# A 256-token hybrid block on one core: diagonal blocks of 32 rows solved on VectorE in place of 16, and side work handed out in larger turns

## The chip, the cores and the metric

One core of a Trainium2 chip runs one launch of the kernel. The metric is the device time of that launch in microseconds. The kernel before has a median of 1571.18 us over 3 runs (1570.76 to 1572.39). Engines are called by the profile's short names: PE is TensorE (PEld its weight load), DVE is VectorE, ACT is ScalarE, POOL is GpSimd, SP is SyncE.

## What is computed

One layer on 256 tokens of width 2048, all in float32. Branch A is a gated delta rule in chunks of 64 rows with 8 heads of width 128; branch B is latent attention with 8 heads; then an output projection, an MLP of width 8192 and a gated embedding. Cut to the part that the change touches:

```python
h = rms_norm(x) ; proj = h @ w_in            # q|k|v|z|beta|alpha, MLA parts, gates
q, k, v = silu(causal_conv(...)) ; q, k = l2norm(q), l2norm(k)
a = where(strict, (k*beta) @ k.T * decay, 0)       # per head and chunk
t_inv = triangular_solve(eye + a, eye)             # lower triangular inverse
w, u = t_inv @ (k*beta*exp(gc)), t_inv @ (v*beta)
# scan over chunks: v_new = u - w @ state; o = q @ state + qk @ v_new; ...
y = sigmoid(g_a) * (o_a @ w_branch_a) + sigmoid(g_b) * (o_b @ w_branch_b)
x = x + y @ w_out
x = x + relu(rms_norm(x) @ w_mlp_up)**2 @ w_mlp_down
x = x + sigmoid(rms_norm(x) @ w_ple_gate) * (p @ w_ple)
```

## The kernel before

**The stream.** Nearly all of PE's time goes to the large weight matrices. `stream` walks through a list of groups; a group is one block of 512 (or fewer) weight columns, and a step is two K tiles of 128 rows of it. Each weight tile is loaded by SP (`raw`, 5 buffers), cut by `cut` into a rounded part `whi` on ACT and a rest `wlo` on DVE (4 buffers each), and used in 12 matmuls per step (L425), or 8 of 512 and 8 of 256 columns in the groups of the up projection (L418 and L421). `cut(i + AHEAD)` with AHEAD = 3 stands at the head of step i, so a cut is written down three steps before its use, and its buffer comes free when the step four before it has been used.

**Side work.** Everything else (convolutions, norms, attention, the delta rule, transposes of activations) is written as generators in four lanes: L_MLA, L_CONV, L_SOLVE, L_TURN. Each `yield` ends a turn. After every step `weave()` is called twice; a call gives one turn to one lane, and a lane gets at most one turn in two calls, so about one per step. Where a step needs activations that are not written yet, `until` hands out turns at once. The order in which the instructions are written down is a priority: once `rx` is known, ACT and DVE are no longer held to it, and the framework puts each engine's instructions in an order by readiness under a model of its own.

**The inverse.** `inverse(half)` works on four heads and both token blocks `tb` of 128 rows (two chunks each). It computes `dt` (decay, bank `gr`) and the transposed `a` in `at`, then inverts I + a by blocks: the diagonal blocks of BASE = 16 rows are solved directly, and LEVELS = (16, 32, 64) doubles the block size three times. For the direct solve, `at` is masked and reduced on DVE to `ri`, sent by POOL's DMA queue to DRAM (`there`) and back as 64 blocks on 64 partitions (`blk`), solved row by row in 15 pairs of a multiply and a reduce on DVE, and sent through DRAM (`back`) to `ro`. At each level and for each tb, DVE makes `full` (tile `d`, the block columns spread over 128 columns) and `off` (tile `n`, masked `at`); PE makes four transposes (bank `te`, L949) and four float32 matmuls (bank `tx`, L954), then four more (bank `td`, L962 or L971); ACT copies `te` to `e` and `tx` to `xx`. A float32 matmul is two instructions on PE, a transpose is one: a turn with `te` and `tx` holds 4 + 8 instructions, a turn with `td` holds 8. `recur(half)` follows with 7 turns of matmuls, and `gated` turns the result into `oaT`, which the four groups of w_branch_a read.

**Buffers.** Tiles made by `big` share 23 slots of 4 KB per partition; PSUM has four banks for the stream (`acc`) and four for side work (`bank`).

**Where the turns end.** Before the change: `Acts.fill` ends a turn after two K tiles (one bank); `attention` after each query block's scores, and after each block's normalization; `conv` after each pair of heads and after each token block; `inverse` after each `gr`, each pair of `kk`, and each tb of each stage of a level. L_SOLVE thus takes 42 turns per half of the heads (6 to `at`, 3 for the way there, 5 for the solve, 3 for the way back, 18 for the levels, 7 for the recurrence).

Of the kernel before, what the change touches and what calls it, by code (L numbers as in the profile page):

```python
# [17 lines left out]
P = 128  # L18
# [19 lines left out]
C_GB = 8272  # L38
BASE = 16
LEVELS = (16, 32, 64)  # L40
NPIECE = 5
# [8 lines left out]
def _constants():  # L50

    i = np.arange(P)
    row, col = i[:, None], i[None, :]
    cols, at, n = [], {}, 0

    def put(name, a):
        nonlocal n
        a = np.broadcast_to(np.asarray(a, np.float32), (P, a.shape[-1]))
        at[name] = (n, n + a.shape[-1])
        n += a.shape[-1]  # L60
        cols.append(a)
# [10 lines left out]
    put("base", ((row // BASE == col // BASE) & (row < col)) * -1.0)  # L72
# [76 lines left out]
def hybrid_block(ctx: ExitStack, tc: tile.TileContext, a, dbg=None):  # L149
# [111 lines left out]
    class Acts:  # L261
# [18 lines left out]
        def fill(self, k0, src, scales=None):  # L280

            for j in range(src.shape[2] // (2 * P)):
# [18 lines left out]
                self.ready.update((k0 + 2 * j, k0 + 2 * j + 1))  # L301
                yield

# [352 lines left out]
    def evac_kv(g, ps):  # L656
# [30 lines left out]
    def attention(g):  # L687
        qn, qr, kn, v = (mla[c][g] for c in ("qn", "qr", "kn", "v"))
        prs = []
        for qb in range(NT):  # L690
# [17 lines left out]
            prs.append(pr)  # L708
            yield
            rs = small(2, "srs")  # L710
            dve.reciprocal(rs, sm)
            for e in range(2):
                dve.tensor_scalar(pr[:, e, :nk], pr[:, e, :nk], rs[:, e : e + 1], None, ALU.mult)
            yield
        pt0 = mid(f"pt0{g}", shape=(P, 2, T))
# [25 lines left out]
    def gates():  # L741
# [19 lines left out]
        for n in (15, 13, 11, 9, 7, 5, 3):  # L761
# [5 lines left out]
                                       ALU.mult, ALU.mult)  # L767
        yield
        ps = bank("gsum")[:, : 6 * NH].rearrange("p (b m h) -> p b m h", b=NT, m=3)
        for tb in range(NT):  # L770
# [15 lines left out]
    def conv(kind, half, ev):  # L786

        acc = big(f"cv{kind}{half}", shape=(P, 4, T))
        for pair in range(2):
# [5 lines left out]
            for e in range(2):  # L795
# [7 lines left out]
            yield  # L803
        y = acc
# [8 lines left out]
        for tb in range(NT):  # L813
# [8 lines left out]
            yield  # L822
        if kind in "qk":
# [8 lines left out]
        if kind in "kv":  # L832
            g[kind] = tm
        if kind == "k":
            kT = y
            for pair in range(2):
# [5 lines left out]
                act.copy(kT[:, 2 * pair : 2 * pair + 2, :].rearrange("p a b -> p (a b)"), tp)  # L842
                yield
            g["kT"] = kT
# [9 lines left out]
    def inverse(half):  # L854

        g = gdn[half]
        kT, qT = g["kT"], g["qT"]
        ats = []
        for tb in range(NT):
# [11 lines left out]
            act.activation(dt, dt, AF.Exp)  # L871
            yield
            at, qk = mid(f"at{half}{tb}"), mid(f"qk{half}{tb}")
            for pair in range(2):
# [6 lines left out]
                for e in range(2):  # L881
# [5 lines left out]
                    dve.tensor_tensor(qk[:, hs], ps[:, (2 * e + 1) * P : (2 * e + 2) * P], dt[:, hs], ALU.mult)  # L887
                yield
            g["qk", tb] = qk
# [8 lines left out]

        nb = P // BASE
# [6 lines left out]
        there = dpool.tile([NT, 4, P, BASE], F32, tag="there", name=f"there{half}")  # L906
        back = dpool.tile([NT, 4, P, BASE], F32, tag="back", name=f"back{half}")
        flat = lambda t: t.rearrange("b h (n j) i -> (b h n) j i", j=BASE)
        room = big(f"blk{half}", shape=(nblk, 3, BASE, BASE))
        blk, sol, prod = room[:, 0], room[:, 1], room[:, 2]  # L910
        for tb in range(NT):
            nc.gpsimd.dma_start(there[tb].rearrange("h p i -> p h i"), rows_in[:, tb])
        nc.gpsimd.dma_start(blk, flat(there))
        dve.memset(sol.rearrange("p i c -> p (i c)"), 0.0)
        dve.memset(sol.rearrange("p i c -> p (i c)")[:, 0 :: BASE + 1], 1.0)
        yield
        yield
# [7 lines left out]
        rows_out = mid(f"ro{half}", shape=(P, NT, 4, BASE), tag="ro", bufs=1)  # L925
        nc.gpsimd.dma_start(flat(back), sol)
        for tb in range(NT):
            nc.gpsimd.dma_start(rows_out[:, tb], back[tb].rearrange("h p c -> p h c"))
        yield
        yield  # L930
        yield


        cols = [rows_out[:, tb] for tb in range(NT)]
        inv_t, off, full, xx = [None] * NT, [None] * NT, [None] * NT, [None] * NT
        for b in LEVELS:
            for tb in range(NT):
                full[tb], off[tb] = mid(f"d{half}{tb}_{b}"), mid(f"n{half}{tb}_{b}")
                for h in range(4):
                    dve.tensor_tensor(  # L940
                        full[tb][:, h * P : (h + 1) * P].rearrange("p (n c) -> p n c", c=b),
                        cols[tb][:, h, :].unsqueeze(1).to_broadcast([P, P // b, b]),
                        C(f"bd{b}").rearrange("p (n c) -> p n c", c=b), ALU.mult)
                dve.tensor_tensor(v4(off[tb]), v4(ats[tb]), mask(f"lv{b}"), ALU.mult)
                yield
            for tb in range(NT):
                tp = bank(f"te{half}{tb}_{b}")
                for h in range(4):
                    pe.transpose(tp[:, h * P : (h + 1) * P], full[tb][:, h * P : (h + 1) * P], ident)  # L949
# [6 lines left out]
                act.copy(xx[tb], ps)  # L956
                yield
            for tb in range(NT):
# [9 lines left out]
                else:  # L968
# [5 lines left out]
                    g["inv_t", tb] = inv_t[tb]  # L974
                yield

# [299 lines left out]
```

## Time and profile before

| | |
|---|---|
| median of 3 runs | 1571.18 us |
| the profiled execution's own time | 1570.8 us |
| its span in the profile | 1569.0 us |
| PE, DVE, ACT, POOL busy in the span | 1559.6, 976.6, 775.7, 11.4 us |
| granted TensorE clock, mean | 0.999 |
| HBM traffic over the span | 181 GB/s |

The profile lists busy times per engine; since matmuls are pipelined, a busy PE says only that something was in flight. The chain of waits names, from the end backwards, what each piece of work followed; its rows give the start, the length and the number of instructions of a piece, and on PE the starts of successive pieces add up without overlap, so that a piece's length there is what it costs. Rows of groups give the count, the busy time of the group and, apart from it, the mean duration of one instruction, which on PE is a latency and longer than its share.

### The profile page before, as it was taken

The numbers are of one execution on the slowest core, as the hardware profiler recorded it, in microseconds if no ns is written. First come the engines' busy times: TensorE is split into PE (matmuls) and PEld (weight loads), VectorE is DVE, ScalarE is ACT, GpSimd is POOL, SyncE is SP. The second block draws the span as 40 slices with busy tenths as digits, with TensorE's granted clock in tenths as the row PEclk, the third lists the DMA queues.
The fourth block names the chain that finished last, engine by engine and source line by source line (L and its number), as shares of the span: only waits on it lengthen the run. The fifth ranks groups of instructions, "written<-read, shape, count | busy, mean of one in ns | idle before, by whom it ended". The sixth has DMA issues, their size and how long they took to land.

```text
span 1569.0 us, 20945 instructions
## 1 busy us (share of the span) xinstructions
PE 1559.6 (99%) x7856; PEld 1319.2 (84%) x7856; DVE 976.6 (62%) x1687; ACT 775.7 (49%) x1190; POOL 11.4 (1%) x23
## 2 busy tenths in 40 slices
PE   9999999999999999999999999999999999999998
PEld 7998888888888888888888888888888888888888
DVE  6987777954784655655665665556554665555554
ACT  6765776644534544444444443344433443445543
POOL 0000000100000000000000000000000000000000
PEclk9999999999999999999999999999999999999999
DMA  8564343444454455655555555555555555555563
GB/s 304 163 197 172 140 154 135 157 161 148 153 189 150 159 188 188 214 203 187 187 188 188 188 188 188 196 191 187 191 188 190 187 184 197 190 185 181 183 205 116
DMA packets 88518, 284.86 MB, mean 182 GB/s; under 512 B 9248, under 2 KB 22176, under 8 KB 88416
## 3 DMA queue, kind: packets, MB, share of 16 engines
q1 hardware_dynamic: 87168, 281.68, 52.6%
q10 hardware_dynamic: 864, 1.32, 0.3%
q8 instruction: 61, 1.00, 0.2%
q0 software_dynamic: 384, 0.53, 0.2%
q14 instruction: 41, 0.34, 0.1%
HBM read 281.13 MB, written 2.36 MB: 181 GB/s over the span
## 4 chain that ended last, share of the span: by engine, by line
PE 93%; DVE 3%; ACT 2%; DMA 1%; issue 1%; DVEq 0%; ACTq 0%
PE ps L425 65%; PE ps L418 15%; PE ps L421 8%; DMA raw<-in_weights 1%; DVE wlo L142 1%; PE tx L954 1%; ACT whi L142 1%; PE td L962 0%; DVE blk L142 0%; PE te L949 0%; DVE cvv L142 0%; ACT junk_k L142 0%; DMA first_x<-in_xT 0%; PE sc L696 0%; PE sc L695 0%
## 5 line engine op out<-in xcount | busy, mean ns | idle before, releaser
L142 DVE TENSOR_TENSOR wlo<-raw,whi 128x1024 fp32r<-128x1024 f32 (+3 forms) x541 | 644.1, 1192 | 499.8 <-ACT whi L142 497.4
L142 ACT CAST whi<-raw 128x1024 fp32r<-128x1024 f32 (+3 forms) x541 | 554.4, 1026 | 724.8 <-PE ps L425 494.7
L425 PE MATMUL ps<-whi,hT 128*128 128x512 f32 (+2 forms) x1344 | 424.1, 387 | 0.0
L425 PE MATMUL ps<-whi,uT 128*128 128x512 f32 x1024 | 320.4, 393 | 0.0
L425 PEld LDWEIGHTS ps<-whi,hT 128*128 128x128 f32 x1344 | 251.2, 188 | 42.5
L418 PE MATMUL ps<-nT,whi 128*128 128x512 f32 x1024 | 279.8, 394 | 0.0
L425 PE MATMUL ps<-wlo,hT 128*128 128x512 f32 (+2 forms) x672 | 256.8, 382 | 0.7 <-DVE wlo L142 0.7
L425 PEld LDWEIGHTS ps<-whi,uT 128*128 128x128 f32 x1024 | 191.9, 188 | 42.6
L425 PE MATMUL ps<-wlo,uT 128*128 128x512 f32 x512 | 200.8, 392 | 0.0
L418 PEld LDWEIGHTS ps<-nT,whi 128*128 128x128 f32 x1024 | 175.2, 188 | 23.1 <-DVE x L142 0.5
L421 PEld LDWEIGHTS ps<-nT,wlo 128*128 128x128 f32 x1024 | 157.1, 188 | 22.2
L421 PE MATMUL ps<-nT,wlo 128*128 128x256 f32 x1024 | 163.4, 281 | 0.0
L425 PEld LDWEIGHTS ps<-wlo,hT 128*128 128x128 f32 x672 | 126.6, 188 | 21.0 <-DVE wlo L142 1.0
L425 PEld LDWEIGHTS ps<-wlo,uT 128*128 128x128 f32 x512 | 96.2, 188 | 21.3
L425 PE MATMUL ps<-whi,gT 128*128 128x512 f32 (+1 forms) x320 | 82.3, 347 | 0.0
L425 PE MATMUL ps<-whi,yT 128*128 128x512 f32 x256 | 80.6, 393 | 0.0
L425 PEld LDWEIGHTS ps<-whi,gT 128*128 128x128 f32 x320 | 56.1, 189 | 7.5
L425 PEld LDWEIGHTS ps<-whi,yT 128*128 128x128 f32 x256 | 47.9, 189 | 9.5
L425 PE MATMUL ps<-wlo,gT 128*128 128x512 f32 (+1 forms) x160 | 55.5, 347 | 0.0
L425 PE MATMUL ps<-wlo,yT 128*128 128x512 f32 x128 | 50.2, 392 | 0.0
L425 PE MATMUL ps<-whi,oaT 128*128 128x512 f32 x128 | 40.7, 394 | 0.0
L425 PE MATMUL ps<-whi,obT 128*128 128x512 f32 x128 | 40.2, 392 | 0.0
(451 smaller groups left out, 1186.8 us busy)
## 6 DMA issues: line engine op xcount, KB each, us to landing
raw<-in_weights SPq DMA_DIRECT2D x492, 512.0 KB, 3.3
raw<-in_weights SPq DMA_DIRECT2D x24, 384.0 KB, 3.4
raw<-in_weights SPq DMA_DIRECT2D x16, 256.0 KB, 3.1
raw<-in_weights SPq DMA_DIRECT2D x7, 464.0 KB, 7.2
x<-in_x SPq DMA_DIRECT2D x4, 512.0 KB, 7.0
xT<-in_xT SPq DMA_DIRECT2D x7, 256.0 KB, 7.0
cst<-in_cst SPq DMA_DIRECT2D x1, 852.5 KB, 7.6
out<-sg SPq DMA_DIRECT2D x3, 256.0 KB, 2.8
```

Of the source, the lines that this page charges most:

```text
L142: i = f(*args, **kwargs)
L418: pe.matmul(ps[c], hi[:, j, cs], g.acts.both(k), start=first, stop=False)
L421: pe.matmul(ps[c][:, :T], lo[:, j, cs], g.acts.both(k)[:, :T], start=False, stop=last)
L425: pe.matmul(ps[tb], g.acts.at(k, part, tb), w[:, j, : g.n], start=(first and n_ == 0), stop=(last and n_ == 2),)
L954: pe.matmul(ps[:, h, :], off[tb][:, h * P : (h + 1) * P], cols[tb][:, h, :], start=True, stop=True)
```

## The change

BASE becomes 32 and LEVELS (32, 64). The direct solve now has 32 blocks of 32 rows; each block's 32 columns are split into four strips of STRIP = 8 columns, which fill 128 partitions. Per half, POOL's queue carries 8 writes of `at`'s diagonal blocks to DRAM, 4 loads (`room`), 4 writes of the result and 2 loads (`turned`), 18 in place of 6. ACT negates and turns the blocks (`flip`), and DVE runs 31 pairs of a multiply and a reduce over 8 columns. The result is transposed in 32x32 blocks by DVE (`cols`), and the spread and masked copy `inv_t` is made from `turned` on DVE, so that level 32 has no transposes on PE and level 16 is gone. The masks, the reduces to `ri` and two clearings are gone too.

Turns are merged: `fill` ends one after four K tiles; `attention` holds both query blocks; `conv` holds both pairs and both token blocks; `inverse` holds both `gr`, both pairs of a `kk`, and both token blocks of `td` and (level 32) of `tx`. One empty turn is added in `gates`, in `conv` of k and, between the normalization and the transposes, in `evac_kv`. L_SOLVE now takes 43 turns per half (1 + 2 to `at`, 5 for the way there, 1 for `flip`, 10 for the solve, 6 for the way back, 2 + 9 for the levels, 7 for the recurrence).

```diff
-BASE = 16
-LEVELS = (16, 32, 64)
+BASE = 32
+LEVELS = (32, 64)
+STRIP = 8
...
                 self.ready.update((k0 + 2 * j, k0 + 2 * j + 1))
-                yield
+                if j % 2 or 2 * j + 2 >= src.shape[2] // P:
+                    yield
...
-        rows_in = mid(f"ri{half}", shape=(P, NT, 4, BASE), tag="ri", bufs=1)
-        for tb in range(NT):
-            d = mid(f"db{half}{tb}")
-            dve.tensor_tensor(v4(d), v4(ats[tb]), mask("base"), ALU.mult)
-            dve.tensor_reduce(rows_in[:, tb], d.rearrange("p (h n c) -> p h c n", h=4, n=nb), AX.X, ALU.add)
...
+        for tb in range(NT):
+            for n in range(nb):
+                ns_ = slice(n * BASE, (n + 1) * BASE)
+                nc.gpsimd.dma_start(there[tb, :, n].rearrange("h j i -> j h i"), v4(ats[tb])[ns_, :, ns_])
+        room = big(f"blk{half}", shape=(P, BASE * BASE))
+        flip = big(f"flip{half}", shape=(P, BASE, BASE))
+        work = big(f"strip{half}", shape=(P, 2, STRIP, BASE))
+        sol, prod = work[:, 0], work[:, 1]
+        for c in range(ns):
+            nc.gpsimd.dma_start(room[c * nblk : (c + 1) * nblk], there.rearrange("b h n j i -> (b h n) (j i)"))
+        unit = C("unit").rearrange("p (c j) -> p c j", j=BASE)
+        act.copy(prod, unit)
+        act.copy(sol[:, :, 0:1], unit[:, :, 0:1])
+        for _ in range(5):
+            yield
+        act.activation(flip, room.rearrange("p (j i) -> p i j", i=BASE), AF.Copy, scale=-1.0)
         yield
         for i in range(1, BASE):
-            dve.tensor_tensor(prod[:, :i, :i], blk[:, :i, i : i + 1].to_broadcast([nblk, i, i]), sol[:, :i, :i],
-                              ALU.mult)
-            dve.tensor_reduce(sol[:, i, :i], prod[:, :i, :i].rearrange("p j c -> p c j"), AX.X, ALU.add)
+            dve.tensor_tensor(prod[:, :, :i], flip[:, i : i + 1, :i].to_broadcast([P, STRIP, i]), sol[:, :, :i], ALU.mult)
+            dve.tensor_reduce(sol[:, :, i : i + 1].rearrange("p c o -> p (c o)"), prod[:, :, : i + 1], AX.X, ALU.add)
             if i % 3 == 0:
                 yield
...
+        for c in range(ns):
+            nc.gpsimd.dma_start(
+                back.rearrange("b h n c j -> (b h n) (c j)")[:, c * STRIP * BASE : (c + 1) * STRIP * BASE],
+                sol[c * nblk : (c + 1) * nblk].rearrange("p c j -> p (c j)"))
+        for tb in range(NT):
+            nc.gpsimd.dma_start(turned[tb], back[tb].rearrange("h n c j -> (n c) h j"))
+        for _ in range(6):
+            yield
...
+            dve.transpose(cols[tb].rearrange("p h c -> p (h c)"), turned[tb].rearrange("p h c -> p (h c)"))
+            inv_t[tb] = mid(f"e{half}{tb}_{BASE}")
+            for h in range(4):
+                dve.tensor_tensor(
+                    inv_t[tb][:, h * P : (h + 1) * P].rearrange("p (n c) -> p n c", c=BASE),
+                    turned[tb][:, h, :].unsqueeze(1).to_broadcast([P, nb, BASE]),
+                    C(f"bd{BASE}").rearrange("p (n c) -> p n c", c=BASE), ALU.mult)
...
-                tp = bank(f"te{half}{tb}_{b}")
-                for h in range(4):
-                    pe.transpose(tp[:, h * P : (h + 1) * P], full[tb][:, h * P : (h + 1) * P], ident)
-                inv_t[tb] = mid(f"e{half}{tb}_{b}")
-                act.copy(inv_t[tb], tp)
+                if b != BASE:
+                    tp = bank(f"te{half}{tb}_{b}")
+                    for h in range(4):
+                        pe.transpose(tp[:, h * P : (h + 1) * P], full[tb][:, h * P : (h + 1) * P], ident)
+                    inv_t[tb] = mid(f"e{half}{tb}_{b}")
+                    act.copy(inv_t[tb], tp)
```

More of the change, by code (lines that the diff above doesn't have):

```diff
@@ L71, in _constants @@
         put(f"lv{b}", same * ((row // b) % 2 == 0) * ((col // b) % 2 == 1) * 1.0)
-    put("base", ((row // BASE == col // BASE) & (row < col)) * -1.0)
+    c, j = np.arange(STRIP * BASE)[None] // BASE, np.arange(STRIP * BASE)[None] % BASE
+    put("unit", (j == STRIP * (row // (P * STRIP // BASE)) + c) * 1.0)
     for b in LEVELS:
@@ L688, in attention @@
         qn, qr, kn, v = (mla[c][g] for c in ("qn", "qr", "kn", "v"))
-        prs = []
+        prs, sums = [], []
         for qb in range(NT):
@@ L708, in attention @@
             prs.append(pr)
-            yield
+            sums.append(sm)
+        yield
+        for qb in range(NT):
+            nk, pr = (qb + 1) * P, prs[qb]
             rs = small(2, "srs")
-            dve.reciprocal(rs, sm)
+            dve.reciprocal(rs, sums[qb])
             for e in range(2):
                 dve.tensor_scalar(pr[:, e, :nk], pr[:, e, :nk], rs[:, e : e + 1], None, ALU.mult)
-            yield
+        yield
         pt0 = mid(f"pt0{g}", shape=(P, 2, T))
@@ L768, in gates @@
         yield
+        yield
         ps = bank("gsum")[:, : 6 * NH].rearrange("p (b m h) -> p b m h", b=NT, m=3)
@@ L802, in conv @@
                                                    ALU.mult, ALU.add)
-            yield
+        yield
         y = acc
@@ L821, in conv @@
                     squares_n(tp[:, h * P : (h + 1) * P], ss[:, tb * 4 + h : tb * 4 + h + 1], HD, f"{kind}{half}{tb}{h}")
-            yield
+        yield
         if kind in "qk":
@@ L834, in conv @@
         if kind == "k":
+            yield
             kT = y
@@ L842, in conv @@
                 act.copy(kT[:, 2 * pair : 2 * pair + 2, :].rearrange("p a b -> p (a b)"), tp)
-                yield
+            yield
             g["kT"] = kT
@@ L857, in inverse @@
         kT, qT = g["kT"], g["qT"]
-        ats = []
+        ats, dts = [], []
         for tb in range(NT):
@@ L871, in inverse @@
             act.activation(dt, dt, AF.Exp)
-            yield
+            dts.append(dt)
+        yield
+        for tb in range(NT):
+            ts, dt = slice(tb * P, (tb + 1) * P), dts[tb]
             at, qk = mid(f"at{half}{tb}"), mid(f"qk{half}{tb}")
@@ L887, in inverse @@
                     dve.tensor_tensor(qk[:, hs], ps[:, (2 * e + 1) * P : (2 * e + 2) * P], dt[:, hs], ALU.mult)
-                yield
+            yield
             g["qk", tb] = qk
@@ L896, in packed @@
             return mid(f"{name}{half}{tb}_{b}", shape=(P, 4, b), tag=name if name == "xx" else f"{name}{b}", bufs=2)
-        nb = P // BASE
+        nb, ns = P // BASE, BASE // STRIP
         nblk = NT * 4 * nb
-        rows_in = mid(f"ri{half}", shape=(P, NT, 4, BASE), tag="ri", bufs=1)
+        there = dpool.tile([NT, 4, nb, BASE, BASE], F32, tag="there", name=f"there{half}")
+        back = dpool.tile([NT, 4, nb, BASE, BASE], F32, tag="back", name=f"back{half}")
         for tb in range(NT):
-            d = mid(f"db{half}{tb}")
-            dve.tensor_tensor(v4(d), v4(ats[tb]), mask("base"), ALU.mult)
-            dve.tensor_reduce(rows_in[:, tb], d.rearrange("p (h n c) -> p h c n", h=4, n=nb), AX.X, ALU.add)
@@ L906, in inverse @@
[L906 to L910, printed above, removed]
-        for tb in range(NT):
-            nc.gpsimd.dma_start(there[tb].rearrange("h p i -> p h i"), rows_in[:, tb])
-        nc.gpsimd.dma_start(blk, flat(there))
@@ L918, in inverse @@
+        sol, prod = work[:, 0], work[:, 1]
[5 more added lines that the diff above has]
+        for _ in range(5):
+            yield
+        act.activation(flip, room.rearrange("p (j i) -> p i j", i=BASE), AF.Copy, scale=-1.0)
         yield
         for i in range(1, BASE):
-            dve.tensor_tensor(prod[:, :i, :i], blk[:, :i, i : i + 1].to_broadcast([nblk, i, i]), sol[:, :i, :i],
-                              ALU.mult)
@@ L922, in inverse @@
-            dve.tensor_reduce(sol[:, i, :i], prod[:, :i, :i].rearrange("p j c -> p c j"), AX.X, ALU.add)
+            dve.tensor_tensor(prod[:, :, :i], flip[:, i : i + 1, :i].to_broadcast([P, STRIP, i]), sol[:, :, :i], ALU.mult)
+            dve.tensor_reduce(sol[:, :, i : i + 1].rearrange("p c o -> p (c o)"), prod[:, :, : i + 1], AX.X, ALU.add)
             if i % 3 == 0:
                 yield
-        rows_out = mid(f"ro{half}", shape=(P, NT, 4, BASE), tag="ro", bufs=1)
-        nc.gpsimd.dma_start(flat(back), sol)
@@ L927, in inverse @@
-        for tb in range(NT):
[L928 to L935, printed above, removed]
+        turned = [mid(f"tr{half}{tb}", shape=(P, 4, BASE), tag="tr", bufs=2) for tb in range(NT)]
+        for c in range(ns):
+            nc.gpsimd.dma_start(
+                back.rearrange("b h n c j -> (b h n) (c j)")[:, c * STRIP * BASE : (c + 1) * STRIP * BASE],
+                sol[c * nblk : (c + 1) * nblk].rearrange("p c j -> p (c j)"))
@@ new lines, in inverse @@
+        for tb in range(NT):
+            nc.gpsimd.dma_start(turned[tb], back[tb].rearrange("h n c j -> (n c) h j"))
+        for _ in range(6):
+            yield
+        inv_t, off, full, xx, cols = [None] * NT, [None] * NT, [None] * NT, [None] * NT, [None] * NT
+        for tb in range(NT):
+            cols[tb] = packed("cols", tb, BASE)
+            dve.transpose(cols[tb].rearrange("p h c -> p (h c)"), turned[tb].rearrange("p h c -> p (h c)"))
[5 more added lines that the diff above has]
+                    C(f"bd{BASE}").rearrange("p (n c) -> p n c", c=BASE), ALU.mult)
+            yield
@@ L936, in inverse @@
         for b in LEVELS:
             for tb in range(NT):
-                full[tb], off[tb] = mid(f"d{half}{tb}_{b}"), mid(f"n{half}{tb}_{b}")
-                for h in range(4):
[L940 to L943, printed above, removed]
+                off[tb] = mid(f"n{half}{tb}_{b}")
@@ L944, in inverse @@
+                if b != BASE:
+                    full[tb] = mid(f"d{half}{tb}_{b}")
+                    for h in range(4):
+                        dve.tensor_tensor(
+                            full[tb][:, h * P : (h + 1) * P].rearrange("p (n c) -> p n c", c=b),
+                            cols[tb][:, h, :].unsqueeze(1).to_broadcast([P, P // b, b]),
+                            C(f"bd{b}").rearrange("p (n c) -> p n c", c=b), ALU.mult)
                 dve.tensor_tensor(v4(off[tb]), v4(ats[tb]), mask(f"lv{b}"), ALU.mult)
@@ L946, in inverse @@
             for tb in range(NT):
-                tp = bank(f"te{half}{tb}_{b}")
-                for h in range(4):
-                    pe.transpose(tp[:, h * P : (h + 1) * P], full[tb][:, h * P : (h + 1) * P], ident)
-                inv_t[tb] = mid(f"e{half}{tb}_{b}")
-                act.copy(inv_t[tb], tp)
+                if b != BASE:
+                    tp = bank(f"te{half}{tb}_{b}")
+                    for h in range(4):
+                        pe.transpose(tp[:, h * P : (h + 1) * P], full[tb][:, h * P : (h + 1) * P], ident)
+                    inv_t[tb] = mid(f"e{half}{tb}_{b}")
+                    act.copy(inv_t[tb], tp)
                 ps = bank(f"tx{half}{tb}_{b}")[:, : 4 * b].rearrange("p (h c) -> p h c", h=4)
@@ L956, in inverse @@
                 act.copy(xx[tb], ps)
-                yield
+                if b != BASE or tb == NT - 1:
+                    yield
             for tb in range(NT):
@@ L974, in inverse @@
                     g["inv_t", tb] = inv_t[tb]
-                yield
+            yield
     o_tm = [None, None]
```

4 lines of the change are left out of this document (removed).

## The prediction

> **What bounds the kernel now.** I read the page first: engine totals, then the chain that ended last.
>
> ```profile
> PE 1559.6 (99%) x7856; PEld 1319.2 (84%) x7856; DVE 976.6 (62%) x1687; ACT 775.7 (49%) x1190; POOL 11.4 (1%) x23
> PE 93%; DVE 3%; ACT 2%; DMA 1%; issue 1%; DVEq 0%; ACTq 0%
> ```
>
> PE is in use for 1559.6 us of a span of 1569.0, and the chain runs through it for 93%. So two things count: what PE no longer issues, and any new time for which it would have to wait. Next, who makes PE wait now, in the list of waits for PE:
>
> ```profile
> PE idle L210 <- POOL spin L205: 1.4, 1, 1.4
> PE xsum L485 <- DVE xsq L142: 1.2, 1, 1.2
> PE ps L425 <- DVE wlo L142: 0.7, 1, 0.7
> PE gsum L772 <- DVE gate L142: 0.6, 1, 0.6
> PE tp_kT L840 <- DVE tmk L142: 0.5, 2, 0.3
> PE tp_tmv L816 <- ACT cvv L142: 0.5, 1, 0.5
> ```
>
> That is the whole list (total, times, longest), 4.9 us; gsum and tp_kT lie where the change adds an empty turn. Then the price of a turn of side work, from the chain in the first half's levels (16, and 32 from 334 us on):
>
> ```profile
> 318.17 0.80 PE tx L954 x8
> 318.97 2.86 PE ps L425 x12
> 321.83 0.80 PE td L962 x8
> 322.63 2.82 PE ps L425 x12
> ...
> 334.52 0.44 PE te L949 x4
> 334.95 0.81 PE tx L954 x8
> 335.77 2.85 PE ps L425 x12
> ```
>
> and from a stretch without any turn, where a step of 12 costs 32.64 / 12 = 2.72 us:
>
> ```profile
> 419.91 32.64 PE ps L425 x144
> ```
>
> **The change, part by part.**
>
> *PE instructions that go.* A turn with te and tx costs 0.44 + 0.80, and its next step 2.86 in place of 2.72: 1.38 us. A turn with td costs 0.80 + (2.82 - 2.72) = 0.90. Level 16 has two of each per half, so 2 x 2 x (1.38 + 0.90) = 9.1 us go. At level 32 four te go, two per half: 4 x 0.44 = 1.8. Together 10.9 us, on the path, since nothing else fills PE's place.
>
> The group rows tempt to another price:
>
> ```profile
> L949 PE MATMUL te<-cst,d 128*128 128x128 f32 x48 | 7.2, 272 | 0.0
> ```
>
> 272 ns is the latency of one; the chain's 0.44 for four says 110 ns each, and I take the chain. The eight instructions of td with 16 columns cost 0.80 us, 100 ns each. Beside this row: the Trainium skill (TensorE: Matmul & The Clock Gate, Back-to-back issue gap) gives about 60 cycles, 25 ns, for a free dimension of 1 to 64. By it the 64 instructions of tx and td at level 16 would be worth 1.6 us and not 6.4, an estimate from that page; the trace does not agree with it here.
>
> *Turns that merge.* Small turns of 4 and 8 instructions:
>
> ```profile
> 392.66 0.89 PE oo L1019 x8
> 393.55 2.76 PE ps L425 x12
> 396.31 0.44 PE gr L864 x4
> 396.74 2.75 PE ps L425 x12
> ```
>
> An instruction costs the same in both (0.11), and the step behind either takes 0.03 to 0.04 more than 2.72. So a merge saves one such return, 0.03. From the diff: fill 15 (cT 1, oaT 2, yT, nT, gT 4 each), attention 4, conv 12, kT 2, gr 2, kk 4, levels 6: 45 merges, 1.35 us. Bounds: 0 (the order is made by readiness, below) to 1.8.
>
> *Empty turns.* One more step (2.72 us) between DVE's work and PE's transposes in gates and conv(k) covers waits of at most 0.6: 1.1 us go. The one in `evac_kv` has no wait to cover. Bounds 0 to 1.1; what would be late next there is nothing that the list shows.
>
> *DVE's work in the solve.* Rows for the pieces:
>
> ```profile
> L142 DVE TENSOR_REDUCE blk<-blk 64x1 f32<-64x1 f32 (+14 forms) x30 | 8.7, 290 | 0.7
> L142 DVE TENSOR_TENSOR blk<-blk 64x1 f32<-64x1 f32 (+14 forms) x30 | 7.1, 236 | 4.0 <-DMA blk<-there 3.3
> ...
> L142 DVE TENSOR_TENSOR n<-at,cst 128x512 f32<-128x512 f32 x12 | 8.2, 684 | 0.0
> L142 DVE TENSOR_REDUCE ri<-db 128x64 f32<-128x512 f32 x4 | 4.0, 1016 | 0.0
> L142 DVE TENSOR_TENSOR d<-ro,cst 128x128 f32<-128x128 f32 x16 | 3.6, 285 | 5.3 <-DMA ro<-back 5.3
> L142 DVE TENSOR_REDUCE smx<-sc 128x2 f32<-128x512 f32 x4 | 2.7, 682 | 0.0
> L142 DVE TENSOR_TENSOR db<-at,cst 128x512 f32<-128x512 f32 x4 | 2.6, 681 | 0.0
> L142 DVE TENSOR_REDUCE smx<-sc 128x2 f32<-128x256 f32 x4 | 1.7, 423 | 0.1
> L142 DVE TENSOR_TENSOR blk<-blk 64x225 f32<-64x225 f32 x2 | 0.8, 384 | 0.0
> ```
>
> ```profile
> 425.56 0.15 DVE L142 TENSOR_TENSOR blk<-blk 64x1 f32<-64x1 f32 x1 [3.31 <-DMA blk<-there]
> ```
>
> A multiply costs 0.15 us with one element and 0.384 with 225, 1.05 ns per element. Row i now has 8i elements, 3968 over 31 rows: 31 x 0.15 + 4.2 = 8.8. A contiguous reduce costs (682 - 423) / 256 = 1.01 ns per element over a base of 0.16; 8(i + 1), 4216 in all: 5.0 + 4.3 = 9.3. Per half 18.1 us. What goes per half: half of 8.7 + 7.1 + 4.0 + 3.6 + 2.6 and of a third of n's 8.2: 14.4. DVE's net is about +4 us per half, and it has 38% of the span idle. I cost it at nothing, hidden beside the stream; without that cover, in the stage where DVE is fullest, up to 7.0 (a rival below). The two 32x32 transposes per half are shown nowhere; by 128 elements per partition they lie between the 0.285 of a d and the 1.016 of a ri, and I take 0.3.
>
> *ACT* loses the copies of te and gains `flip`, 1024 elements: as a whi, 1.05 us (row below). Nothing on the path.
>
> *Slots and turns.* `flip` and `work` take two more of the 23 slots of `big`. Counted in the code, the second half's solve finds hT 8, obT 4, its own 4, the gates 4 and o 1 = 21, and wants 3: one tile may have to wait until the last w_branch_b group lets go of obT, about a dozen steps. L_SOLVE has 43 turns per half for 42. I cost both at nothing: what reads the result, oaT, comes after two z and four g_a groups, 48 steps; without those steps it would be a dozen steps of waiting.
>
> *DMAs on POOL's queue, and who waits for them.* This is where new waiting can come from, because the readers stand in order in their engines' queues, with weight cuts behind them:
>
> ```profile
> 443.32 0.55 POOL L926 DMA_DIRECT2D back<-blk  x1 [20.69 <-DVE blk L142]
> ```
>
> ```profile
> 442.95 2.34 DVE L142 TENSOR_TENSOR wlo<-raw,whi 128x1024 fp32r<-128x1024 f32 x2
> ...
> 450.57 0.90 DVE L142 TENSOR_TENSOR d<-ro,cst 128x128 f32<-128x128 f32 x4 [5.27 <-DMA ro<-back]
> ...
> 451.99 1.22 DVE L142 TENSOR_TENSOR wlo<-raw,whi 128x1024 fp32r<-128x1024 f32 x1
> ```
>
> ```profile
> 447.14 1.05 ACT L142 CAST whi<-raw 128x1024 fp32r<-128x1024 f32 x1 [1.66 <-PE ps L425]
> ```
>
> DVE stood still for 5.27 us on the way back and cut no weights from 445.29 to 451.99, 6.7 us; yet the 144 matmuls above run unbroken to 452.55. The cushion is the three steps of AHEAD: the cut whose whi started at 447.14 is used 3 x 2.72 later, at 455.3, and was done at 453.2. So 2.1 us were left. The yields do not prevent such a wait: the order is made by readiness in the framework's model, which put the reader too early. After the change three more writes precede the loads (3 x 0.55 = 1.65) and the transpose comes on top (0.3): 1.95 of the 2.1. On the way there DVE waited 3.31; now ACT's `flip` waits, with three more writes of the last tb and three more loads: 3.31 + 6 x 0.55 = 6.6. Behind it a whi is late by 6.6 + 1.05 - 1.66 = 6.0, and what it has in hand is 455.3 - (447.14 + 1.05 + 1.22) = 5.9. All four places end at the edge of the cushion. Each costs from 0 up to its whole wait (6.6 or 5.27 + 1.65 = 6.9, 27 us in all); the nearest row, the one that cost PE nothing, says near 0. I take 0.6 each: 2.4 us.
>
> *Sum.* 1570.8 - 10.9 - 1.35 - 1.1 + 2.4 = 1559.85 for the profiled execution. The median lies 0.4 above it: 1560.3.
>
> **The rivals.**
>
> *The cushion is already spent (slower).* In the first half the solve falls among the convolutions:
>
> ```profile
> 275.00:314.00 39.00, 38.54 (x185) 31.25 (x184) 35.84 (x93) 25.09 (x45) 4.29 (x6) 1.00 0.49 156
> ```
>
> (span, PE, PEld, DVE, ACT and POOL busy.) DVE is busy for 35.84 of 39 us, so cuts may run late before a wait begins. If both waits of a half reach PE in full, 13.5 us are lost: 1559.85 + 13.5 - 1.2 + 0.4 = 1572.6 for one half, no change; for both, 1584.9, slower. It decides once over 13.35 us of the 27 reach PE. For it: the queue now holds 18 DMAs per half. Against: the second half's row, where DVE stood still and PE did not. 0.08 and 0.05.
>
> *DVE becomes the bound in that stage.* There the solve replaces about 7.9 us by 18.1, and only 39 - 35.84 = 3.2 are free: 10.2 - 3.2 = 7.0 too much, 1567.3. Against it: the work that goes with it (14.4) lies nearby, and the solve has ten turns to spread over, not five. The Trainium skill (VectorE: DVE Perf Modes, Rules for kernel authors) calls tensor_reduce the slowest DVE operation and advises to restructure; the rows here give it 1.01 ns per element against a multiply's 1.05, so I add no chance for that. 0.10.
>
> *The merges are only priorities.* PE's order is by readiness, so turns split again:
>
> ```profile
> 623.29 0.27 PE L287 MATMUL tp_yT__6103<-cst,gb 128*128 128x128 f32 x1
> 623.87 0.49 PE L287 MATMUL tp_yT__6103<-cst,gb 128*128 128x128 f32 x3
> ```
>
> Four transposes of one turn stand here as 1 + 3. If merges and empty turns bring nothing, 1560.3 + 2.45 = 1562.8. 0.10.
>
> *Small instructions cost 25 ns,* the rule above: 4.8 us less gain, 1565.1. The td row speaks against it: 0.02.
>
> **How the numbers follow.** The forecast, 1560.3, has 0.65 (its own range 1556 to 1564); the rivals have 0.08, 0.05, 0.10, 0.10 and 0.02. 0.2% is 3.1 us, about what a measurement can tell from no change: faster is below 1568.0. That holds for the forecast and for the last three rivals: 0.87; the one-half case is the same, 0.08; slower 0.05. The range is 1556 (no new waits and merges at 1.8 give 1557.4; the rest is for waits of the list that I left in) to 1568, which takes in all faster cases.
>
> **What would show it.** Right: te with 16 instructions in place of 48, no tx or td with 16 columns, and steps behind turns still at 2.75 to 2.86; DVE's total about 8 us up; waits of PE on gate and tmk gone; DMA waits of ACT at `flip` and DVE at the transposes of 5 to 8 us with PE's chain unbroken beside them. Wrong: PE waiting for wlo or whi by more than 3 us in all, or a chain that leaves PE for POOL's DMAs; or level-32 turns that cost more than their 0.11 per instruction.

## The result

The changed kernel takes 1561.05 us (median of 6 runs, 1559.55 to 1562.76) beside 1571.70 for the kernel before (6 runs, 1570.76 to 1572.40): a ratio of 0.9933, 95% interval 0.9920 to 0.9945, so 8.6 to 12.6 us less. The forecast was 1560.3. A second measurement on another chip (after_again, beside the kernel before on that chip) gave 1560.83 and a ratio of 0.9921 (0.9907 to 0.9934). The profiled execution of the first took 1560.76 us with a span of 1559.0, 10.0 less than before. One execution of the run merged_only below took 5071 us, and its ratio leaves it out. In the changed kernel's rows L428 is the stream's matmul (L425 before), and L144 the helper of DVE and ACT (L142 before).

Engine totals and the chain by engine, from the page of the changed kernel:

```profile
PE 1548.6 (99%) x7760; PEld 1310.6 (84%) x7760; DVE 979.6 (63%) x1715; ACT 772.8 (50%) x1182; POOL 22.8 (1%) x47
PE 97%; DVE 2%; ACT 1%; issue 0%; POOL 0%; DVEq 0%; ACTq 0%; POOLq 0%
```

PE is in use for 11.0 us less, with 96 instructions fewer. DVE has only 3.0 us more, POOL twice its former work, and no DMA is left in the chain. The list of waits for PE (total, times, longest):

```profile
PE tp_kT L849 <- DVE tmk L144: 1.6, 1, 1.6
PE xsum L488 <- DVE xsq L144: 1.5, 1, 1.5
PE idle L212 <- POOL spin L207: 1.4, 1, 1.4
PE tp_kn L681 <- DVE kn L144: 0.6, 1, 0.6
PE gsum L780 <- DVE gate L144: 0.6, 1, 0.6
```

The list is no shorter than before: 5.7 us for 4.9. gsum stands where it stood, tp_kT has grown from 0.5 to 1.6. Next the price of the turns that stayed, in the chain of the first half's levels:

```profile
330.96 2.81 PE ps L428 x12
333.77 1.70 PE td L990 x16
335.48 8.25 PE ps L428 x36
343.73 0.44 PE te L976 x4
344.17 0.84 PE tx L981 x8
```

A merged turn of 16 costs 1.70, 0.106 per instruction, and the step behind it 2.81: an instruction's price is what the prediction took, in turns of any size. On DVE, the groups of the new solve, and ACT's `flip`:

```profile
L144 DVE TENSOR_REDUCE strip<-strip 128x8 f32<-128x16 f32 (+30 forms) x62 | 18.2, 294 | 1.1
L144 DVE TENSOR_TENSOR strip<-flip,strip 128x8 f32<-128x8 f32 (+30 forms) x62 | 18.1, 292 | 4.4 <-ACT flip L144 3.1
L144 ACT ACTIVATE flip<-blk 128x1024 f32<-128x1024 f32 x2 | 4.3, 2136 | 0.0
```

That is 18.15 us per half, for 18.1 predicted. `flip` waited for nothing ("0.0"), but took 2.14 us, not 1.05, and DVE waited for `flip`: 3.1 of the 4.4 us at the end of the second row. Last the place that the prediction feared most, the way back in the second half: DVE's rows, then PE's beside them.

```profile
447.01 1.23 DVE L144 TENSOR_TENSOR wlo<-raw,whi 128x1024 fp32r<-128x1024 f32 x1 [0.40 <-ACT whi L144]
453.86 0.31 DVE L144 STREAM_TRANSPOSE cols<-tr 128x128 f32<-128x128 f32 x1 [5.62 <-DMA tr<-back]
...
455.67 1.22 DVE L144 TENSOR_TENSOR wlo<-raw,whi 128x1024 fp32r<-128x1024 f32 x1
```

```profile
456.38 0.61 PE L428 MATMUL ps<-whi,hT 128*128 128x512 f32 x2
456.94 0.50 PE L428 MATMUL ps<-wlo,hT 128*128 128x512 f32 x1
457.28 0.62 PE L428 MATMUL ps<-whi,hT 128*128 128x512 f32 x2
```

DVE stood for 5.62 us and cut no weights from 448.24 to 455.67, 7.43 us. PE's starts, 0.227 apart otherwise, slipped once: the two whi and the wlo that follow take 0.56 and 0.34 in place of 0.45 and 0.23, so 0.22 us were paid. In the second profile of the same kernel (after_again) DVE stood there for 6.64 us, and PE had to wait for the cut:

```profile
459.91 0.50 PE L428 MATMUL ps<-wlo,hT 128*128 128x512 f32 x1 [0.97 <-DVE wlo L144]
```

### The profile page after: what moved, and what is told of

Same layout as the page of the kernel before. It is cut to its first block, busy times and chain, and to the rows that moved or that the text cites. A ratio compares the mean times of both kernels' runs of the same rounds, so it can differ in the third digit from the quotient of the medians.

```text
span 1559.0 us, 20821 instructions
## 1 busy us (share of the span) xinstructions
PE 1548.6 (99%) x7760; PEld 1310.6 (84%) x7760; DVE 979.6 (63%) x1715; ACT 772.8 (50%) x1182; POOL 22.8 (1%) x47
## 4 chain that ended last, share of the span: by engine, by line
PE 97%; DVE 2%; ACT 1%; issue 0%; POOL 0%; DVEq 0%; ACTq 0%; POOLq 0%
PE ps L428 68%; PE ps L421 15%; PE ps L424 8%; DVE wlo L144 1%; PE tx L981 0%; PE idle L212 0%; PE sc L699 0%; PE sc L700 0%; DVE strip L144 0%; ACT whi L144 0%; PE vn L1029 0%; PE kk L891 0%; PE oo L1047 0%; PE kk L890 0%; DVE xsq L144 0%
## 5 line engine op out<-in xcount | busy, mean ns | idle before, releaser
L144 DVE TENSOR_TENSOR wlo<-raw,whi 128x1024 fp32r<-128x1024 f32 (+3 forms) x541 | 644.1, 1192 | 487.6 <-ACT whi L144 484.7
L144 ACT CAST whi<-raw 128x1024 fp32r<-128x1024 f32 (+3 forms) x541 | 554.5, 1026 | 710.9 <-PE ps L428 492.2
L428 PE MATMUL ps<-whi,hT 128*128 128x512 f32 (+2 forms) x1344 | 418.5, 386 | 0.0
L428 PE MATMUL ps<-whi,uT 128*128 128x512 f32 x1024 | 319.4, 392 | 0.0
L428 PEld LDWEIGHTS ps<-whi,hT 128*128 128x128 f32 x1344 | 251.8, 189 | 43.1
L428 PE MATMUL ps<-wlo,hT 128*128 128x512 f32 (+2 forms) x672 | 257.9, 384 | 0.0
L428 PEld LDWEIGHTS ps<-whi,uT 128*128 128x128 f32 x1024 | 192.0, 188 | 42.8
L428 PE MATMUL ps<-wlo,uT 128*128 128x512 f32 x512 | 201.0, 393 | 0.0
L428 PEld LDWEIGHTS ps<-wlo,hT 128*128 128x128 f32 x672 | 126.8, 189 | 21.3 <-DVE wlo L144 0.4
L428 PEld LDWEIGHTS ps<-wlo,uT 128*128 128x128 f32 x512 | 96.1, 188 | 21.4
L428 PE MATMUL ps<-whi,gT 128*128 128x512 f32 (+1 forms) x320 | 82.3, 347 | 0.0
L428 PE MATMUL ps<-whi,yT 128*128 128x512 f32 x256 | 79.7, 391 | 0.0
L428 PEld LDWEIGHTS ps<-whi,gT 128*128 128x128 f32 x320 | 56.1, 189 | 7.5
L428 PEld LDWEIGHTS ps<-whi,yT 128*128 128x128 f32 x256 | 47.8, 188 | 9.7
L428 PE MATMUL ps<-wlo,gT 128*128 128x512 f32 (+1 forms) x160 | 55.5, 347 | 0.0
L428 PE MATMUL ps<-wlo,yT 128*128 128x512 f32 x128 | 50.1, 392 | 0.0
L428 PE MATMUL ps<-whi,oaT 128*128 128x512 f32 x128 | 40.7, 394 | 0.0
L428 PE MATMUL ps<-whi,obT 128*128 128x512 f32 x128 | 39.5, 389 | 0.0
```

The costliest lines, as they stand in the source:

```text
L144: i = f(*args, **kwargs)
L428: pe.matmul(ps[tb], g.acts.at(k, part, tb), w[:, j, : g.n], start=(first and n_ == 0), stop=(last and n_ == 2),)
```

## The experiments

Theory: the gain is PE's instructions at 0.11 us each, and the merges give what their returns cost. Rival: the merges carry it, or the gain of the solve is partly eaten by the waits it brings. Each run was timed beside the kernel before on the same chip; the ratios below are to that. The runs stand in three groups on three chips, on which the kernel before took 1573.15, 1574.35 and 1573.19 us, so runs of different groups are compared by their ratios: solve_only to xsum_later are the first group, xsum_strip, after_again, no_empty and hop_twice the second, and no_empty_tx, hop_strip_tx and strip_kT the third.

**solve_only.** The new solve, with the turns of the kernel before:

```diff
-                if b != BASE or tb == NT - 1:
-                    yield
+                yield
...
-            yield
+                yield
```

(and so at every place where the change merged or added turns.)

> The new solve (blocks of 32 rows, level 16 gone, no transposes at level 32) with the turns of the kernel before. Theory P (the gain is the PE instructions that go, 0.11 us each): 10.9 us below the kernel before, about 1560.8, and te, tx and td group counts as in the changed kernel. Rival M (the merged turns bring the gain and the solve's DMA waits eat what PE saves): within 3 us of the kernel before. Rival Z (merging is worth nothing): equal to the changed kernel, 1561.0, within 0.5.

1561.51 us for 1573.15, ratio 0.9927 (0.9915 to 0.9940): 9.4 to 13.4 us less. The solve alone brings the whole gain, as far as the intervals can tell, and rival M falls. Theory P and rival Z forecast nearly the same time for this run, which does not tell them apart.

**merged_only.** The merged and the empty turns, with the solve of the kernel before (blocks of 16, levels 16, 32, 64).

> The merged and the empty turns of the change with the old solve of 16 rows. Theory P: 45 returns to the stream at 0.03 us are saved, 1.35 us, about 1570.3; the empty turns bring nothing. Rival M: 5 us or more below the kernel before. Rival Z: equal to it, 1571.7 within 0.5. Rival L (larger turns wait longer for DVE and ACT): 1 us or more above it, with new waits of PE in the list.

1571.58 us, ratio 0.9989 (0.9980 to 0.9998): 0.3 to 3.1 us less. The merges, taken together with the empty turns, are worth something, the 1.35 predicted lies within, and they do not carry the result.

**te_back.** The changed kernel, with e at level 32 made by PE's transposes and ACT's copies again:

```diff
-                if b != BASE:
+                if True:
                     tp = bank(f"te{half}{tb}_{b}")
```

> The changed kernel with level 32's transposes back on PE (16 of them, 4 more per token block in the same turns) and DVE making the spread copy from the transposed columns. Theory P: 16 x 0.11 = 1.8 us above the changed kernel, about 1562.8, with tx turns at level 32 of 24 instructions in place of 16. Rival (transposes in a turn that is there anyway hide behind it): 1561.0, no change.

1562.73 us, ratio 0.9932 (0.9920 to 0.9944). The chain of this kernel has the instructions back at their price:

```profile
328.19 0.44 PE te L970 x4
328.63 0.81 PE tx L975 x8
329.44 0.47 PE te L970 x4
```

By the distance from each PE instruction's start to the next, its te cost 1.82 us more in all, for the 1.8 of the sum. In the total times 1.8 us cannot be told from nothing between two groups of runs.

**xsum_later.** A step that the prediction had not looked at: in the profiles of before and after, PE waits at xsum. Before first, then after:

```profile
37.95 0.61 PE L485 MATMUL xsum<-ones,xsq 128*128 128x2 f32 x4 [1.18 <-DVE xsq L142]
38.42 0.48 PE L425 MATMUL ps<-whi,hT 128*128 128x512 f32 x1
38.73 0.40 PE L425 MATMUL ps<-wlo,hT 128*128 128x512 f32 x1
```

```profile
37.40 0.61 PE L488 MATMUL xsum<-ones,xsq 128*128 128x2 f32 x4 [1.54 <-DVE xsq L144]
37.87 0.78 PE L428 MATMUL ps<-whi,hT 128*128 128x512 f32 x1
38.44 0.63 PE L428 MATMUL ps<-wlo,hT 128*128 128x512 f32 x1
```

After the longer wait the matmuls take about 0.43 us each in place of 0.23, eight of them, until 41.37: some 1.6 us on top of the wait, at a lower clock (granted 0.50 from 37.88 to 41.29). So the changed kernel got one more empty turn ahead of xsum:

```diff
         yield
+        yield
         ps = bank("xsum")
```

> The changed kernel with one more empty turn ahead of the sum over squares at 37 us, where its profile shows PE waiting 1.5 us and eight matmuls after it at half the clock. Theory C (the wait costs 1.5 us and the lowered clock behind it another 1.6): about 3 us below the changed kernel, 1558, no wait on xsq in PE's list, and a granted clock of 1.00 in the first 45 us. Rival (PE waits for the same value at the next place, the evacuation of the first group): 1561, with the wait under another name. Rival (the clock falls there anyway): 1559.5.

1571.71 us, ratio 0.9993 (0.9984 to 1.0001). The expectation fell. The wait at xsum was gone and the early clock full, and yet the whole gain was lost. ACT's and PE's rows in the second half:

```profile
443.56 2.12 ACT L144 ACTIVATE flip<-blk 128x1024 f32<-128x1024 f32 x1 [1.66 <-PE ps L428]
```

```profile
492.49 1.92 PE L982 MATMUL tx<-cols,n 128*128 128x32 f32 x8 [5.90 <-DVE n L144]
494.21 0.77 PE L428 MATMUL ps<-wlo,hT 128*128 128x512 f32 x1
494.79 0.63 PE L428 MATMUL ps<-whi,hT 128*128 128x512 f32 x1
```

In the changed kernel this `flip` starts at 406.08. Here one more turn at the start put a gb of the gates ahead of it, and a slot of `big` was missing. Judged by the time of its start, `flip` got the slot of the first obT tile: the last w_branch_b group begins at 440.6 and is done with that tile a step later, at 443.4. The solve ended at 479.1, 36 us later than the 443.2 of the changed kernel. PE came to tx before its operand was there, waited 5.90, and then ran to 507 at 0.43 us per matmul, again at the lower clock (granted 0.50 from 489.77 to 506.84). The prediction had counted this slot (21 of 23 held, 3 wanted) and costed it at nothing.

**xsum_strip.** To tell the slot from the DMA wait on DVE, which stood in xsum_later as well (5.79 us): `strip` is 2 KB and need not hold a 4 KB slot.

```diff
-        work = big(f"strip{half}", shape=(P, 2, STRIP, BASE))
+        work = mid(f"strip{half}", shape=(P, 2, STRIP, BASE))
```

> xsum_later with one edit: the tile of `strip` (512 elements per partition) is taken from the 2 KB tiles and no longer from the 4 KB slots of `big`. Slot theory (what cost xsum_later its 10 us is one slot of `big` that the second half's `flip` had to wait for, until the last w_branch_b group let go of obT; so the solve ended 36 us later, at 479, and its result was not there when PE came to the levels): flip is back near 406, the solve ends near 442, no wait of PE at tx, none at xsum, no lowered clock at either place, and the time is 1558 (the changed kernel's time less 1.5 for the xsum wait and 1.5 for the clock after it). Rival, cushion theory (the 5.8 us for which DVE stood at the DMA are themselves what PE paid in xsum_later): the DMA wait is still there, so PE still waits 4 to 6 us at tx or wlo, and the time stays at 1568 to 1572.

1558.43 us (1558.38 to 1559.71), ratio 0.9903 (0.9888 to 0.9918). The slot theory holds: `flip` is at 409.06, PE has no wait at tx, and DVE still waits 10.2 us in all for the DMA. Its list of waits for PE:

```profile
PE tp_kT L850 <- DVE tmk L144: 2.2, 2, 1.8
PE idle L212 <- POOL spin L207: 1.4, 1, 1.4
PE ps L428 <- DVE wlo L144: 0.8, 2, 0.6
PE gsum L781 <- DVE gate L144: 0.6, 1, 0.6
PE ptA L728 <- DVE l2qu L144: 0.4, 1, 0.4
```

This version beats both kernels; the changed kernel, run in the same group (after_again), took 1560.83.

> The changed kernel unaltered, as the yardstick for the others of this group. All theories: ratio to the kernel before 0.993, so 9.8 to 11 us less.

**no_empty.** The changed kernel without its three empty turns.

> The changed kernel without its three empty turns (gates, evac_kv, conv of k). The prediction's step (an empty turn takes away the waits at gsum and tp_kT): 1.1 us slower than the changed kernel. My reading of the traces (these waits stood at 0.6 and 1.6 with the empty turns in, so they cover nothing): the same within 0.6 us, with the waits at gsum and tp_kT at 0.6 and 0.5 to 2.

1566.26 us, ratio 0.9953 (0.9940 to 0.9965): 5.4 slower than the changed kernel in the same group. Both expectations fell. The waits at gsum (0.6) and tp_kT (1.9) are near the changed kernel's (0.6 and 1.6), so the empty turns do not cover them; but the turns behind them come in another order, and in the first half PE is at tx too early:

```profile
330.36 1.05 PE L978 MATMUL tx<-cols,n 128*128 128x32 f32 x8 [1.77 <-DVE n L144]
332.10 1.05 PE L978 MATMUL tx<-cols,n 128*128 128x32 f32 x8 [0.69 <-DVE n L144]
332.99 0.48 PE L428 MATMUL ps<-whi,hT 128*128 128x512 f32 x1
333.30 0.43 PE L428 MATMUL ps<-wlo,hT 128*128 128x512 f32 x1
333.53 1.05 PE L428 MATMUL ps<-whi,hT 128*128 128x512 f32 x2
```

2.46 us of waiting, and then two matmuls in 1.05 where they take 0.62, until 336.9.

**no_empty_tx.** The same, with one empty turn put back just ahead of that tx.

```diff
                 dve.tensor_tensor(v4(off[tb]), v4(ats[tb]), mask(f"lv{b}"), ALU.mult)
                 yield
+            if b == BASE:
+                yield
```

> no_empty with one empty turn between the masks of the levels and the products tx of level 32, so that PE comes to tx a step (2.72 us) later. Wait theory (what no_empty lost is PE waiting for n at tx, 2.5 us, and the lowered clock behind it, some 3 us): no wait at tx, no lowered clock in 240 to 340 us, and the time is back at 1560.5 to 1562. Rival (the empty turns were worth their 5 us in other places, the later start of the solve or the order of the side work): the wait at tx goes, 1.8 us at most, and the time stays at 1564 to 1566.

1562.78 us, ratio 0.9937 (0.9924 to 0.9949). The wait at tx is gone and the clock of 240 to 340 us is full again. By the ratios some 2.5 of the 5.4 us are back, but the two intervals overlap, so the times alone do not settle it. In the profiles, counted from the first matmul of the stream, PE is 4.4 us earlier than in no_empty at 400 us, nearly the 2.5 of waiting and 1.7 of clock. In the second half part of it is lost again: DVE stands at the transposes for 6.88 us, and PE waits 1.21 for cut weights, for 0.50 in no_empty.

**hop_twice.** The changed kernel with a longer way back, two further transfers ahead of the transposes:

```diff
-            nc.gpsimd.dma_start(turned[tb], back[tb].rearrange("h n c j -> (n c) h j"))
+            nc.gpsimd.dma_start(hop[tb], back[tb].rearrange("h n c j -> (n c) h j"))
+        for tb in range(NT):
+            nc.gpsimd.dma_start(again[tb].rearrange("h n c j -> (n c) h j"), hop[tb])
+        for tb in range(NT):
+            nc.gpsimd.dma_start(turned[tb], again[tb].rearrange("h n c j -> (n c) h j"))
```

> The changed kernel with a longer way back: the solution goes from memory to a tile, back to memory and to a tile again before it is transposed, so two further transfers stand behind the two there were (7.2 us for two in the changed kernel: some 7 us more until the transposes can start). One or two more cuts of weights stand ahead of the waiting transpose in DVE's order. Cushion theory (the three steps of AHEAD were spent but for a little: a gap of 7.43 us between two cuts cost PE 0.2): the gap grows to some 11 or 12 us and PE pays 4 to 5 us of it in each half, 8 to 10 in all, with some us of lowered clock behind: 1569 to 1575. Rival (the cushion is deeper than the three steps, because the ring of raw and cut tiles runs ahead): PE pays under 1 us, 1561 to 1562.

1567.91 us, ratio 0.9960 (0.9947 to 0.9972): 7.1 slower than the changed kernel. From the waits of its DVE and of its PE:

```profile
DVE cols L144 <- DMA tr<-again: 15.2, 2, 7.9
```

```profile
PE tx L987 <- DVE n L144: 2.4, 2, 1.7
...
PE ps L428 <- DVE wlo L144: 1.2, 2, 0.7
```

DVE waits 15.2 us, for 10.3 in the changed kernel, and now PE pays: 2.4 for the operand of tx in the first half, with the clock at 0.50 from 331.13 to 337.95 behind it, which costs another 3.4, and 0.66 for cut weights in the second. (The other 0.51 of the wlo row lies at 10.6 us, at the start of the stream, where the kernel before has 0.68.) The rival, a deeper cushion, falls. But the time is also below the cushion theory's 1569 to 1575: of the loss some 5.8 us lie at tx, where neither theory looked, and some 1.4 at the cuts.

**hop_strip_tx.** The same, with the empty turn ahead of tx, and `strip` in the 2 KB tiles.

> hop_twice with the same empty turn ahead of tx, and with `strip` in the 2 KB tiles as in xsum_strip (the added turn would otherwise cost `flip` of the second half its slot). Wait theory: the transfers are as long as in hop_twice and DVE waits for them as long, 7 to 8 us in each half, but PE has no wait at tx: 1561 to 1563. Cushion theory, as the prediction has it (PE runs out of cut weights while DVE waits): PE still waits, now for wlo, and the time stays at 1566 to 1568.

1567.35 us, ratio 0.9965 (0.9951 to 0.9978): the cushion theory's figure, but in the main not for its reason. Where the added turn removed the wait at tx, in the first half, PE ran out of cut weights instead:

```profile
329.65 0.50 PE L428 MATMUL ps<-wlo,hT 128*128 128x512 f32 x1 [1.23 <-DVE wlo L144]
...
332.31 1.87 PE L989 MATMUL tx<-cols,n 128*128 128x32 f32 x16
```

DVE had stood for 7.66 us there, and PE loses 1.6 us more here than in the changed kernel. In the second half the wait at tx stayed, 1.63 and 0.66, with the clock at 0.50 from 473.82 to 480.64: 5.7 us more than in the changed kernel. So the wait theory's condition, no wait at tx, was met in the first half alone, and there the cushion theory holds; in the second half the run does not decide between them.

**strip_kT.** xsum_strip with a second empty turn ahead of the transposes of kT.

> xsum_strip with a second empty turn in the convolution of k ahead of the transposes of kT. If another step covers what is left of the wait at tp_kT (2.2 us with one empty turn) without moving other waits: 1556 to 1557. Rival (the wait moves with the turn, since DVE's work ahead of it is put in order by the same turns): 1558.4 again, with 1 to 2 us of wait at tp_kT or elsewhere.

1558.36 us, ratio 0.9909 (0.9895 to 0.9922), the same as xsum_strip, with 1.8 us still at tp_kT. The rival holds: one more step there covers nothing. What the trace suggests as the reason is in the next section.

## Why the prediction was right, step by step

The total was right to 0.8 us and the mechanism too: PE's own instructions set the end, and fewer of them shortened it. Inside the sum the first two terms stand, the second only as far as it can be measured. The next two were wrong, one of them through a misread row, and a cost was missing; these errors partly cancelled, so that the total came so close is in part luck.

- **Instructions that go, 10.9: right.** By the distances from start to start, te, tx and td cost 10.1 us less (1.0 of the 10.9 was to come from the steps behind them). solve_only gives 9.4 to 13.4 for this step alone. Small instructions cost 0.10 to 0.11 and not 0.025: that rival falls.
- **Merges, 1.35: right as far as it can be measured** (merged_only: 0.3 to 3.1). The steps of the stream are 1.3 us shorter in sum, but waits and the lowered clock lie in that sum and the rest of the side work is 1.4 longer, so the two profiles alone do not show this term. That they were only priorities, the rival at 0.10, is not excluded by the lower end of 0.3, but nothing speaks for it.
- **Empty turns, 1.1: failed.** "Covers waits of at most 0.6" took the wait for something that a step's distance covers. It is set by DVE's order, and the solve stands in that order. This is the chain that ends in tp_kT in the changed kernel:

```profile
278.38 0.22 DVE strip L144
278.60 0.08 DVE l2ky L144
278.68 0.22 DVE strip L144
278.90 0.08 DVE rk L144
278.98 0.10 DVE strip L144
...
279.12 0.69 DVE tmk L144
...
279.95 0.41 PE tp_kT L849 x2
```

  Between the small steps of the norm of k, each of 0.08, stand those of the solve, each of 0.2: the solve's instructions were put among those that PE waits for. It is the rival *DVE becomes the bound* in small, at one place, and it costs 1.1 us and not 7.0. That the new solve is the cause is read from this chain and not tested: 1.1 us of waiting stand at tp_kT in solve_only, and in merged_only, which has the old solve, as well. In all, the listed waits went up by 0.8 instead of down by 1.1. (Before's list holds 0.7 for wlo at 11 us, which comes and goes: the changed kernel's second profile has 0.69 there.) What the empty turns were worth lay elsewhere: without them the kernel took 5.4 us more, and no_empty's profile shows 2.5 of waiting and 1.7 of clock at tx.
- **DVE's work, +4 per half at no cost: the size was off, the cover held.** The solve took its 18.15 per half, but DVE's total rose by 3.0 in all. The groups show what was left out of the count: the d of level 32 (16 of 32 d<-cols went, 4.0 us) and the two updates of cols<-ro (2.1); on the other side the 3.5 of e<-tr were not counted either, and the rest of the difference stays open. In the crowded stretch of the first half:

```profile
275.00:314.00 39.00, 37.44 (x180) 30.61 (x180) 38.09 (x110) 22.95 (x43) 1.97 (x4) 1.00 0.46 153
```

  DVE is busy for 38.09 of 39 us, for 35.84 before: fuller, as feared, and PE still goes on but for the 1.56 at tp_kT.
- **The four DMA waits, 2.4: mis-sized, 0.2 in one profile and some 1.2 in the other.** On the way there no engine waited for the DMA: five yields were enough, and `flip` found its data, in both halves. DVE waited 3.1 us for `flip` itself, and PE paid nothing for that. Here the prediction moved the old wait of 3.31 to the new reader without asking when that reader would come. On the way back DVE waited 4.64 and 5.62 (3.86 and 6.64 in after_again), not 6.9, and PE paid 0.22 (0.97 and a slip of some 0.2). The cushion was misread. Counting cuts and steps from the start, the cut of 451.99 to 453.21 in the kernel before belongs to the whi of 444.42, not to that of 447.14, and its first use is this matmul of the kernel before:

```profile
453.95 0.39 PE L425 MATMUL ps<-wlo,obT 128*128 128x512 f32 x1
```

  So 0.74 us were left and not 2.1. In the changed kernel the gap between the two cuts grew by just that, from 6.7 to 7.43, and not by 1.95; in after_again it was 8.45. Two misjudged sizes stood against each other, so the small cost is luck too. With 7.2 to 7.9 us of waiting at each place, some 2 to 3 us more, hop_twice and hop_strip_tx lost 5 to 7 us, most of it at tx. So the wait must also be held against the first side work that reads the result, and what PE waits can be paid again in clock.
- **Slots, nothing: right for this kernel, by the order of two allocations.** xsum_later lost 9.4 us against the changed kernel by the ratios, 10.7 between the two profiled executions. A term costed at nothing on the count "wants 3, finds 2" was the most dangerous of the list.
- **The early lowered clock, not foreseen,** +1.6 in the profiled execution. It is not the change's alone: solve_only, without any merge, shows it too (wait of 1.7 at xsum, mean clock 0.96 in the first 45 us), te_back does not (1.7 and 1.00). Of the 39 executions of the kernel before that were timed beside the experiments, 12 have a mean granted clock of 0.998 or less, and one such spell takes 0.001. Whether the change makes it more frequent stays open.

For the profiled execution, with the predicted figures of the first two terms and the measured ones of the others: -10.9 - 1.35 + 0.8 + 0.2 + 1.6 = -9.65, for the 10.0 that the span shows. Of what was said to show it right, the counts (te 16, no tx or td of 16 columns), the steps of 2.81, and the chain of PE, unbroken but for 0.22, came true; the 8 us on DVE, the vanished waits, and the wait at `flip` did not.

## What to carry to other kernels

On a path that is one engine's instructions, price an edit by start-to-start distances in the chain: that term was good to 0.8 us in the profiles. What is costed at nothing because "something hides it" needs a count of slots and of DVE's order at the one place where PE next reads the result: there one to three turns more or less, far ahead, moved the time by 5 to 11 us. A tile that is smaller than its slot should not hold one when slots run short; taken out, the same turn that had cost 9 to 11 us gained 2.4.

## What the runs showed of the hardware

- PE's clock fell by half after some short waits, for whole windows of 3.41 us. In all thirteen traces the granted clock changes only at whole multiples of 3.413 us after its first rise; in the changed kernel it is 0.50 for one window, from 37.88 to 41.29, where matmuls of 128x512 took 0.43 in place of 0.227. The spell was one window after 1.54 us at xsum and after 1.77 and 0.69 at tx in no_empty, two around the 1.71 and 0.69 at tx in hop_twice, and five, 17.07 us, from within the 5.90 at tx in xsum_later. So a wait of 1.5 to 2.5 us can cost about twice its length.
- Its length alone doesn't decide. At xsum, six waits of 1.54 to 1.80 us that lay in one window (one of them but for 0.15) were each followed by a spell; three that a border between windows split (1.53 and 0.19 in te_back, 1.17 and 0.27 in hop_twice, 0.67 and 0.95 in hop_strip_tx) were not, nor was the 1.18 of the kernel before. But 1.56 to 1.79 within one window at tp_kT lowered nothing, and in after_again the clock also fell from 58.97 to 62.38, behind 0.59 at gsum and its 12 matmuls of 8 columns. What the window counts stays open.
- The Trainium skill (TensorE: Matmul & The Clock Gate, Part 1: The HAM clock gate) has a clock that is halved by a monitor with a free-running window of some 3.4 us: the 0.50 and the 3.41 us agree with that. That a wholly idle window is needed does not agree with 1.54 and 1.77, and the 14 us for which the clock stayed low after PE's return at 492.49 in xsum_later are longer than the one busy window that the page names.
- From start to start an instruction of te, tx or td costs 0.10 to 0.11 us behind a weight tile of 128 columns, whether it moves 16, 32, 64 or 128 columns. The td of the last level, with a weight tile of 64 columns, cost 0.08 before and 0.07 in the changed kernel.
- A 32x32 transpose of 128 elements per partition on DVE takes 0.31 us (0.30 was the estimate); ACT's `flip`, which reads its 1024 elements with a stride, takes 2.14 where a plain cast of 1024 takes 1.05.
- The way back through memory (two transfers, the second waiting for the first) takes 10.7 us in the second half, from the solve's last instruction (ends at 443.15) to the transpose (453.86); in after_again it took 11.7. With two transfers more it takes 15.8 (447.88 to 463.64 in hop_twice): 5.1 us for a further round, of which DVE's wait shows only 2.3, since one more cut stood ahead of the reader.
